# A hybrid decoder step: a hand-written order for the first stage, the first norm in column groups, and moved steps of the final norm

## The chip, the cores and the metric

One core of one Trainium2 chip, a program in Bass with the Tile framework. The time is device time in microseconds of one execution; the median of three runs of the kernel before is 1126.55 us (1126.41 to 1127.04). Engines: TensorE (PE), VectorE (DVE), ScalarE (ACT), GpSimd (POOL), SyncE (SP, which here only issues DMAs).

## What is computed

One layer, for 1024 prompt tokens and 8 x 8 sample tokens, 1088 columns in all; features lie on partitions, tokens in columns.

```
h = RMSNorm(x, g1);  proj = h @ w_in                  # 1024 -> 2816 + 8 columns (dt)
A = gelu(u) * (tril(W_s) gelu(v) + b)                 # chunks of 128 tokens
B = bgate * conv3(cgate * hb)
C = RMSNorm(ssd(silu(conv4(xbc)), softplus(dt)) * silu(z))
x = x + concat(A, B, C) @ w_out
x = x + relu(RMSNorm(x, g2) @ w_ff1)^2 @ w_ff2        # 1024 -> 4096 -> 1024
y = RMSNorm(x, final_norm)
```

## The kernel before, in words

Each float32 operand is split into a high part (a cast to fp32r) and a low part (what is left), and a product is three matmuls: high x high, low x high, high x low (`mm3`, L125 to L130, and `mm_tile`, L1039 to L1046). Columns go in chunks `CH` of 364, 364 and 360, later in quarters of 272.

**First stage.** Eight tiles of x^T (`xts`, 544 KB each) are loaded on SP's queue. For each k, `dt_products(k)` (L240) gives the eight dt columns, the high part of `g1 * x` is made on VectorE for k below 3 and on ScalarE above (L254, L256), the low part on VectorE (L259), the square on ScalarE (`square`, L229), and VectorE adds the squares up in `ss` (`add_square`, L233). The weight of an output tile is split by `split_w` (cast on ScalarE, L97; low part on VectorE, L98). The product of the first weight tile, over all three chunks at once, is L333 and L337. Its result goes to `cb` unscaled (L342). The second weight's `gemm` (L128 to L130) goes chunk by chunk; its first chunk has a PSUM tile of its own, and a hook behind it calls `rms_scale` (L155 to L181): three products of `ones` with `ss` (L169), Ln, Exp and one Newton step on all 1088 columns (L170 to L180), which gives `rstd` on all partitions. After that each result is multiplied with `rstd` when it leaves PSUM (`evac_pad`, L290), and so are the first tile's (L351) and dt (L355, L357). `dt_tokens` (L379) is hooked into the third weight's product, behind its first chunk. PSUM pool `gp` has three banks for the chunks.

**Order.** The text of the program is not the order on the engines: outside `manual_schedule` blocks a planner orders each engine's instructions by its own costs and due times, and fills gaps with later work that is ready. Inside a `manual_schedule(engines=...)` block the named engines run in the written order. In the kernel before there is one such block, around `last_products` (L1346 to L1349), for PE, DVE, ACT and POOL.

**Output projection.** `proj_out(t, f)` (L843) for two halves of the tokens and eight output tiles f, 48 matmuls each; `next_w` splits the weight one tile ahead. During the second half, behind the projections f = 1 to 4, the first half's norm is worked in: `norm_quarter(b, 0, ...)` (L904, four products of 544 columns on VectorE, L909) and `first_operand(n)` (L946, a split into a third of `big`, L914 and L915, and a write to DRAM on SP's queue). `first_operand(0)` needs only quarter (0, 0), `first_operand(1)` needs quarter (1, 0).

**The tail.** `last_products` (L1349) does the last second-layer product by column tiles and the final norm at once. `tile(c, j, m)` is six matmuls of 272 columns on TensorE, `put` (an addition into x on VectorE, L944) and a `square` on ScalarE (L1444). The tokens are done in three parts ci: 0 is the first half, 2 and 3 are quarters. For each part: `rms_mm` (sums of the squares over partitions, L870, four column groups of 32), `root_of` (Sqrt and Identity on ScalarE, L877 and L878; reciprocal and three more on VectorE, L879 to L882), `spread` (L893) of the row to all partitions, a copy of it on ScalarE (L1393, L1468), and the outputs: `weigh` (ScalarE, L1479) followed by `scale` on GpSimd (L1488) for f = 1, 5, 7, and `scale` on VectorE straight out of PSUM (L1493) for the others. `sum_2` and `sum_3` share a PSUM bank. A second product into `ca[m]` can begin only when the first one's `put` has read it.

Of the kernel before, what the change touches and what calls it, by code (L numbers as in the profile page):

```python
# [15 lines left out]
P = 128  # L16
# [52 lines left out]
def body(nc, tc, I, O):  # L69
# [24 lines left out]
    def split_w(st, cuts=(0, 1024), pool=None):  # L94
        w = (pool or whlp).tile([P, 2, 1024], F32R, name="whl")
        for a, b in zip(cuts, cuts[1:]):
            S.copy(out=w[:, 0, a:b], in_=st[:, a:b])  # L97
            V.tensor_tensor(out=w[:, 1, a:b], in0=st[:, a:b], in1=w[:, 0, a:b].bitcast(F32),  # L98
                            op=ALU.subtract)
        return w  # L100
# [9 lines left out]
    def w_split(i):  # L110
        if i < len(w_plan) and i not in w_sp:
            w_sp[i] = split_w(w_st[i], HC if i == 0 else (0, 1024))
# [134 lines left out]
    for k in range(KT):  # L247
        xt = xts[k]
        dt_products(k)
        b = big[:, k * 2 * T:(k + 1) * 2 * T].rearrange("p (h t) -> p h t", h=2)  # L250
        g = C("g1")[:, k:k + 1]
        for a, e in (((0, 364), (364, T)) if k == 0 else ((0, T),)):
            if k > 2:
                S.activation(out=b[:, 0, a:e], in_=xt[:, a:e], func=AF.Identity, scale=g)  # L254
            else:
                V.tensor_scalar(out=b[:, 0, a:e], in0=xt[:, a:e], scalar1=g, scalar2=None, op0=ALU.mult)  # L256
        if k == 0:
            w_split(0)
        V.scalar_tensor_tensor(out=b[:, 1], in0=xt[:, :T], scalar=g, in1=b[:, 0].bitcast(F32),  # L259
                               op0=ALU.mult, op1=ALU.subtract)  # L260
        if k:
            square(k - 1)
        if k > 2:
            add_square(k - 2)
        xg.append(b)
    w_split(1)
    square(KT - 1)
    add_square(KT - 2)
    add_square(KT - 1)
# [22 lines left out]
    S.copy(out=ones, in_=C("ones"))  # L292
# [47 lines left out]
    for c in range(3):  # L340
        for o, i, tok in pad_parts(buf, 3, ps0[c], c):
            S.copy(out=o, in_=i)  # L342
    dtT = tmpp.tile([P, T], F32, name="dtT", tag="t")[:, :DTQ + 32]
    S.copy(out=dtT[:, :DTQ], in_=psd[:, :DTQ])
    S.copy(out=dtT[:64, DTQ:], in_=psd[:64, DTQ:DTQ + 32])
    buf5 = new_buf(3, C("sst")[:, 5 * 24:6 * 24])
    gemm(next_w(), xg, range(KT), lambda c, ps: evac_pad(c, ps, buf5, 3),
         first=ap.tile([P, 512], F32, name="aps", tag="a"), hooks=[lambda: rms_scale(aslots(), catp, "yb", ss, rstd, D, False)])
    for c in range(3):
        for o, i, tok in pad_parts(buf, 3, ps0[c], c):  # L350
            V.tensor_tensor(out=o, in0=o, in1=tok(rstd), op=ALU.mult)  # L351
    conv_c(4, buf)
    for j in range(4):
        r = slice(32 * j, 32 * j + 32)
        V.tensor_tensor(out=dtT[r, :DTQ], in0=dtT[r, :DTQ], in1=rstd[r, j * DTQ:(j + 1) * DTQ], op=ALU.mult)  # L355
        if j < 2:
            V.tensor_tensor(out=dtT[r, DTQ:], in0=dtT[r, DTQ:], in1=rstd[r, SEQ + 32 * j:SEQ + 32 * j + 32],  # L357
                            op=ALU.mult)
    conv_c(5, buf5)
# [100 lines left out]
    V.tensor_tensor(out=ss, in0=rstd, in1=rstd, op=ALU.mult)  # L460
# [592 lines left out]
    for f in range(KT):  # L1053
# [12 lines left out]
        elif f == 2:  # L1066
            norm_quarter(1, 0, two(rstd[:, :NH]))
        elif f == 3:
            first_operand(0)
        elif f == 4:  # L1070
            first_operand(1)
# [277 lines left out]
    def last_products(fo, put):  # L1349
# [37 lines left out]
        for m in range(3):  # L1387
# [9 lines left out]
        tile(0, 3, 3)  # L1397
        scale(0, (0,))
        tile(1, 5, 0)
        rms_mm(2, sum_2)  # L1400
        scale(0, (2,))
        rs[2] = root_of(2, sum_2)
        tile(1, 5, 1)
# [5 lines left out]
        scale(0, (4,))  # L1409
        tile(1, 3, 1)  # L1410
# [4 lines left out]
        weigh(2, (1,))  # L1415
        tile(1, 3, 3)
        weigh(2, (5, 7))
# [198 lines left out]
```

## Time and profile before

| | |
|---|---|
| median of three runs | 1126.55 us |
| the profiled execution | 1127.05 us, span 1125.3 us |
| PE busy | 1111.0 us (99%) |
| DVE busy | 840.4 us (75%) |
| ACT busy | 497.8 us (44%) |
| POOL busy | 53.2 us (5%) |

Times in the rows are microseconds from the span's start. A matmul's time is pipelined: the next one starts before the last one's end. A name in the form L98 is a line of the kernel before. In a timeline row, what stands in square brackets is how long the engine sat idle before, and what it waited for.

### The profile page before, as it was taken

Reading aid. Unit: us, or ns where it says so; the run is one execution under the profiler, and the core shown is the slowest. Engines: PE = TensorE matmul, PEld = TensorE weight load, DVE = VectorE, ACT = ScalarE, POOL = GpSimd, SP = SyncE. Lnnn points to the kernel's source line nnn. Section 1 sums busy time; section 2 is a strip of 40 time slices with the busy share of each in tenths; the row PEclk is TensorE's granted clock in tenths of the full one; section 3 lists DMA queues with packets and bytes.
Section 4 is the critical chain, followed back from the end, with each engine's and each line's share of the span. In section 5 each row is a group of like instructions: output and inputs, shape, how many; then the busy total and the mean of one; then the engine's idle time right before and its main releaser. Section 6 shows DMA issues by size and latency. Waiting matters only on the chain.

```text
span 1125.3 us, 19943 instructions
## 1 busy us (share of the span) xinstructions
PE 1111.0 (99%) x8524; PEld 1090.8 (97%) x8524; DVE 840.4 (75%) x1111; ACT 497.8 (44%) x659; POOL 53.2 (5%) x89
## 2 busy tenths in 40 slices
PE   8999999999999999999999999999999999999996
PEld 6999999999999999999999999999999999999995
DVE  8875587865655477999697497596596596599786
ACT  7536273423553344653343443443443442543544
POOL 1110021110000000000000000000000000000014
PEclk9999999999999999999999999999999999999999
DMA  6112233321027263692853953953953953953504
GB/s 257 52 60 62 61 113 104 114 70 52 34 93 280 79 229 117 277 410 80 336 175 129 399 180 138 390 185 138 394 180 144 382 186 146 378 183 142 215 1 160
DMA packets 34776, 200.43 MB, mean 178 GB/s; under 512 B 4736, under 2 KB 7680, under 8 KB 27776
## 3 DMA queue, kind: packets, MB, share of 16 engines
q1 hardware_dynamic: 32592, 196.30, 47.2%
q10 hardware_dynamic: 2096, 2.85, 0.7%
q8 instruction: 67, 1.10, 0.4%
q14 instruction: 21, 0.17, 0.0%
HBM read 175.58 MB, written 22.77 MB: 176 GB/s over the span
## 4 chain that ended last, share of the span: by engine, by line
PE 94%; DVE 3%; issue 1%; ACT 1%; DMA 1%; POOL 0%; SPq 0%; POOLq 0%; DVEq 0%; ACTq 0%
PE ps L1045 20%; PE ps L1044 20%; PE ps L1046 20%; PE gps L128 10%; PE gps L129 9%; PE gps L130 9%; PE aps L574 1%; PE aps L578 1%; DMA xt<-xT 1%; DVE big L259 1%; DVE xq L909 0%; PE aps L509 0%; PE aps L505 0%; PE p L1044 0%; PE aps L767 0%
## 5 line engine op out<-in xcount | busy, mean ns | idle before, releaser
L1045 PE MATMUL ps<-big,whl 128*128 128x272 f32 x1312 | 377.7, 288 | 0.0
L1044 PE MATMUL ps<-big,whl 128*128 128x272 f32 x1312 | 377.5, 288 | 0.0
L1046 PE MATMUL ps<-big,whl 128*128 128x272 f32 x1312 | 376.9, 287 | 0.0
L1045 PEld LDWEIGHTS ps<-big,whl 128*128 128x128 f32 x1312 | 247.1, 188 | 0.2 <-issue 0.2
L1044 PEld LDWEIGHTS ps<-big,whl 128*128 128x128 f32 x1312 | 247.1, 188 | 0.2
L1046 PEld LDWEIGHTS ps<-big,whl 128*128 128x128 f32 x1312 | 246.8, 188 | 0.0
L128 PE MATMUL gps<-big,whl 128*128 128x360 f32 (+2 forms) x752 | 239.8, 319 | 0.5 <-ACT cb L342 0.5
L129 PE MATMUL gps<-big,whl 128*128 128x360 f32 (+2 forms) x752 | 236.8, 315 | 0.5 <-DVE whl L98 0.5
L130 PE MATMUL gps<-big,whl 128*128 128x360 f32 (+2 forms) x752 | 236.0, 314 | 0.0
L97 ACT CAST whl<-wq 128x1024 fp32r<-128x1024 f32 x92 | 96.6, 1051 | 220.7 <-PE ps L1046 132.9
L98 DVE TENSOR_TENSOR whl<-wq,whl 128x1024 fp32r<-128x1024 f32 x92 | 112.3, 1220 | 50.1 <-ACT whl L97 50.1
L128 PEld LDWEIGHTS gps<-big,whl 128*128 128x128 f32 x752 | 141.4, 188 | 2.0 <-ACT cb L342 1.0
L129 PEld LDWEIGHTS gps<-big,whl 128*128 128x128 f32 x752 | 141.4, 188 | 1.1 <-DVE whl L98 0.7
L130 PEld LDWEIGHTS gps<-big,whl 128*128 128x128 f32 x752 | 141.3, 188 | 0.1
L944 DVE TENSOR_TENSOR x<-x,ps 128x544 f32<-128x544 f32 x188 | 130.5, 713 | 7.8 <-PE ps L1046 6.7
L1046 PE MATMUL ps<-fo,whl 128*128 128x272 f32 x416 | 119.5, 287 | 0.0
L1044 PE MATMUL ps<-fo,whl 128*128 128x272 f32 x416 | 119.3, 287 | 0.0
L1045 PE MATMUL ps<-fo,whl 128*128 128x272 f32 x416 | 119.2, 287 | 0.0
L97 ACT CAST whl<-wst 128x1024 fp32r<-128x1024 f32 (+2 forms) x39 | 40.1, 1027 | 129.5 <-PE gps L130 81.0
L1044 PEld LDWEIGHTS ps<-fo,whl 128*128 128x128 f32 x416 | 78.3, 188 | 0.2 <-issue 0.2
L1046 PEld LDWEIGHTS ps<-fo,whl 128*128 128x128 f32 x416 | 78.2, 188 | 0.0
L1045 PEld LDWEIGHTS ps<-fo,whl 128*128 128x128 f32 x416 | 78.2, 188 | 0.0
(327 smaller groups left out, 1382.1 us busy)
## 6 DMA issues: line engine op xcount, KB each, us to landing
big<-xcd SPq DMA_DIRECT2D x47, 2176.0 KB, 9.7
wq<-w SPq DMA_DIRECT2D x66, 512.0 KB, 4.5
xcd<-big SPq DMA_DIRECT2D x7, 2176.0 KB, 8.1
wst<-w_in SPq DMA_DIRECT2D x21, 512.0 KB, 3.6
wst<-w_out SPq DMA_DIRECT2D x16, 512.0 KB, 3.6
x<-xT SPq DMA_DIRECT2D x8, 544.0 KB, 5.4
dec<-scr SPq DMA_DIRECT2D x8, 512.0 KB, 4.1
xt<-xT SPq DMA_DIRECT2D x7, 544.0 KB, 9.0
```

The source lines that it names most:

```text
L97: S.copy(out=w[:, 0, a:b], in_=st[:, a:b])
L98: V.tensor_tensor(out=w[:, 1, a:b], in0=st[:, a:b], in1=w[:, 0, a:b].bitcast(F32), op=ALU.subtract)
L128: PE.matmul(ps[:, :n], hi, xh, start=start, stop=False)
L129: PE.matmul(ps[:, :n], lo, xh, start=False, stop=False)
L130: PE.matmul(ps[:, :n], hi, xl, start=False, stop=stop)
L259: V.scalar_tensor_tensor(out=b[:, 1], in0=xt[:, :T], scalar=g, in1=b[:, 0].bitcast(F32), op0=ALU.mult, op1=ALU.subtract)
L574: PE.matmul(yps[hh * HD:(hh + 1) * HD, i * L:(i + 1) * L], w[:, h * HD:(h + 1) * HD], m[:, h], start=i == 0 and n == 0, stop=n == len(term ...
L578: PE.matmul(sps[:, g * 256:(g + 1) * 256], bt[:, g * P:(g + 1) * P], xw[:, g * 256:(g + 1) * 256], start=True, stop=True)
L944: V.tensor_tensor(out=out, in0=a, in1=b, op=o)
L1044: PE.matmul(o, hi, xh, start=start and k == 0, stop=False, skip_group_check=True)
L1045: PE.matmul(o, lo, xh, start=False, stop=False, skip_group_check=True)
L1046: PE.matmul(o, hi, xl, start=False, stop=k == ks - 1, skip_group_check=True)
```

## The change

1. First stage: VectorE and ScalarE are put in a `manual_schedule` block. All dt products stand first in the text; then high and low parts, with the sums of squares after the last low part except the square of k = 0 and 1; the second weight's split stands behind `add_square(1)` and `square(2)`. The copies of dt out of PSUM close the block.
2. First norm: the sums go as four column groups of 32 partitions with 364 columns each (the fourth repeats the third), Ln, Exp and the Newton step run on 364 columns, and three products with a column of `ident` spread the result over all partitions, behind the third chunk. The second weight's evacuations come after that; the scaling of dt stands ahead of that of the first tile.
3. The square of `rstd` goes from VectorE to ScalarE.
4. `first_operand(0)` stands behind projection 2 and `norm_quarter(1, 0)` behind projection 3, the reverse of before.
5. Tail: `tile(0, 3, 3)` ahead of the first spread; the sums of part 2 in two pieces, the second and `root_of(2)` behind `tile(1, 5, 1)`; the three weighings of part 2 together, behind `tile(1, 3, 0)`.

```diff
@@ -91,8 +91,9 @@
         SY.dma_start(out=st, in_=src)
         return st
 
-    def split_w(st, cuts=(0, 1024), pool=None):
-        w = (pool or whlp).tile([P, 2, 1024], F32R, name="whl")
+    def split_w(st, cuts=(0, 1024), pool=None, w=None):
+        if w is None:
+            w = (pool or whlp).tile([P, 2, 1024], F32R, name="whl")
         for a, b in zip(cuts, cuts[1:]):
             S.copy(out=w[:, 0, a:b], in_=st[:, a:b])
             V.tensor_tensor(out=w[:, 1, a:b], in0=st[:, a:b], in1=w[:, 0, a:b].bitcast(F32),
@@ -109,7 +110,7 @@
 
     def w_split(i):
         if i < len(w_plan) and i not in w_sp:
-            w_sp[i] = split_w(w_st[i], HC if i == 0 else (0, 1024))
+            w_sp[i] = split_w(w_st[i])
 
     def next_w():
 
@@ -245,28 +246,50 @@
                       start=k == 0 and o == 0, stop=k == KT - 1, skip_group_check=True)
 
     for k in range(KT):
-        xt = xts[k]
-        dt_products(k)
-        b = big[:, k * 2 * T:(k + 1) * 2 * T].rearrange("p (h t) -> p h t", h=2)
+        xg.append(big[:, k * 2 * T:(k + 1) * 2 * T].rearrange("p (h t) -> p h t", h=2))
+
+    def high(k):
         g = C("g1")[:, k:k + 1]
         for a, e in (((0, 364), (364, T)) if k == 0 else ((0, T),)):
+            o, i = xg[k][:, 0, a:e], xts[k][:, a:e]
             if k > 2:
-                S.activation(out=b[:, 0, a:e], in_=xt[:, a:e], func=AF.Identity, scale=g)
+                S.activation(out=o, in_=i, func=AF.Identity, scale=g)
             else:
-                V.tensor_scalar(out=b[:, 0, a:e], in0=xt[:, a:e], scalar1=g, scalar2=None, op0=ALU.mult)
-        if k == 0:
-            w_split(0)
-        V.scalar_tensor_tensor(out=b[:, 1], in0=xt[:, :T], scalar=g, in1=b[:, 0].bitcast(F32),
-                               op0=ALU.mult, op1=ALU.subtract)
-        if k:
-            square(k - 1)
-        if k > 2:
-            add_square(k - 2)
-        xg.append(b)
-    w_split(1)
-    square(KT - 1)
-    add_square(KT - 2)
-    add_square(KT - 1)
+                V.tensor_scalar(out=o, in0=i, scalar1=g, scalar2=None, op0=ALU.mult)
+
+    def low(k):
+        V.scalar_tensor_tensor(out=xg[k][:, 1], in0=xts[k][:, :T], scalar=C("g1")[:, k:k + 1],
+                               in1=xg[k][:, 0].bitcast(F32), op0=ALU.mult, op1=ALU.subtract)
+
+
+    ET = mybir.EngineType
+    with tc.manual_schedule(engines={ET.DVE, ET.Activation}):
+        for k in range(KT):
+            dt_products(k)
+        high(0)
+        low(0)
+        w_sp[0] = whlp.tile([P, 2, 1024], F32R, name="whl")
+        split_w(st0, HC[:2], w=w_sp[0])
+        square(0)
+        high(1)
+        low(1)
+        split_w(st0, HC[1:], w=w_sp[0])
+        high(2)
+        square(1)
+        low(2)
+        for k in range(3, KT):
+            high(k)
+            low(k)
+        add_square(1)
+        square(2)
+        w_split(1)
+        for k in range(2, KT):
+            if k > 2:
+                square(k)
+            add_square(k)
+        dtT = tmpp.tile([P, T], F32, name="dtT", tag="t")[:, :DTQ + 32]
+        S.copy(out=dtT[:, :DTQ], in_=psd[:, :DTQ])
+        S.copy(out=dtT[:64, DTQ:], in_=psd[:64, DTQ:DTQ + 32])
 
     def evac_mul(c, ps, dst, rhs=None):
         rhs = rstd if rhs is None else rhs
@@ -289,7 +312,6 @@
         for o, i, tok in pad_parts(buf, pad, ps, c):
             V.tensor_tensor(out=o, in0=i, in1=tok(rhs), op=ALU.mult)
 
-    S.copy(out=ones, in_=C("ones"))
     stC = sml.tile([P, 8, 27], F32, name="stC")
     xcS = sml.tile([P, 8, TS], F32, name="xcS")
     mids = {}
@@ -340,22 +362,45 @@
     for c in range(3):
         for o, i, tok in pad_parts(buf, 3, ps0[c], c):
             S.copy(out=o, in_=i)
-    dtT = tmpp.tile([P, T], F32, name="dtT", tag="t")[:, :DTQ + 32]
-    S.copy(out=dtT[:, :DTQ], in_=psd[:, :DTQ])
-    S.copy(out=dtT[:64, DTQ:], in_=psd[:64, DTQ:DTQ + 32])
+    S.copy(out=ones, in_=C("ones"))
     buf5 = new_buf(3, C("sst")[:, 5 * 24:6 * 24])
-    gemm(next_w(), xg, range(KT), lambda c, ps: evac_pad(c, ps, buf5, 3),
-         first=ap.tile([P, 512], F32, name="aps", tag="a"), hooks=[lambda: rms_scale(aslots(), catp, "yb", ss, rstd, D, False)])
-    for c in range(3):
-        for o, i, tok in pad_parts(buf, 3, ps0[c], c):
-            V.tensor_tensor(out=o, in0=o, in1=tok(rstd), op=ALU.mult)
-    conv_c(4, buf)
+
+    GRP = ((0, 364), (364, 364), (724, 364), (724, 364))
+    nrm = catp.tile([P, T], F32, name="nrm", tag="yb")
+    nr, nt = nrm[:, :364], nrm[:, 364:728]
+
+    def norm_sums():
+        sb = ap.tile([P, 512], F32, name="aps", tag="a")[:, :364]
+        for j, (c0, n) in enumerate(GRP):
+            PE.matmul(sb[32 * j:32 * j + 32], C("ones")[:, :32], ss[:, c0:c0 + n], start=True, stop=True,
+                      skip_group_check=True)
+        S.activation(out=nt, in_=sb, func=AF.Ln, bias=C("eps"), scale=1.0 / D)
+        V.tensor_scalar(out=sb, in0=sb, scalar1=1.0 / D, scalar2=EPS, op0=ALU.mult, op1=ALU.add)
+        S.activation(out=nr, in_=nt, func=AF.Exp, scale=-0.5)
+        V.tensor_tensor(out=nt, in0=nr, in1=nr, op=ALU.mult)
+        V.scalar_tensor_tensor(out=nt, in0=nt, scalar=-0.5, in1=sb, op0=ALU.mult, op1=ALU.mult)
+        V.scalar_tensor_tensor(out=nr, in0=nt, scalar=1.5, in1=nr, op0=ALU.add, op1=ALU.mult)
+
+    def norm_spread():
+        for j, (ps, (c0, n)) in enumerate(zip(aslots(), CH)):
+            PE.matmul(ps[:, :364], C("ident")[:, 32 * j:32 * j + 1].broadcast_to([P, P]), nr, start=True, stop=True)
+            S.copy(out=rstd[:, c0:c0 + n], in_=ps[:, 364 - n:364])
+
+    held = []
+    gemm(next_w(), xg, range(KT), lambda c, ps: held.append((c, ps)), first=ap.tile([P, 512], F32, name="aps", tag="a"),
+         hooks=[norm_sums, lambda: None, norm_spread])
+    for c, ps in held:
+        evac_pad(c, ps, buf5, 3)
     for j in range(4):
         r = slice(32 * j, 32 * j + 32)
         V.tensor_tensor(out=dtT[r, :DTQ], in0=dtT[r, :DTQ], in1=rstd[r, j * DTQ:(j + 1) * DTQ], op=ALU.mult)
         if j < 2:
             V.tensor_tensor(out=dtT[r, DTQ:], in0=dtT[r, DTQ:], in1=rstd[r, SEQ + 32 * j:SEQ + 32 * j + 32],
                             op=ALU.mult)
+    for c in range(3):
+        for o, i, tok in pad_parts(buf, 3, ps0[c], c):
+            V.tensor_tensor(out=o, in0=o, in1=tok(rstd), op=ALU.mult)
+    conv_c(4, buf)
     conv_c(5, buf5)
 
 
@@ -457,7 +502,7 @@
 
     stB = sml.tile([P, 2, 18], F32, name="stB")
     catB = []
-    V.tensor_tensor(out=ss, in0=rstd, in1=rstd, op=ALU.mult)
+    S.activation(out=ss, in_=rstd, func=AF.Square)
 
     def proj_b(i):
         cg = tmpp.tile([P, T], F32, name="cg", tag="t")
@@ -1064,9 +1109,9 @@
                 S.copy(out=rstd[:, CQ[c]], in_=ps[:, :NQ])
             norm_quarter(0, 0, two(rstd[:, :NH]))
         elif f == 2:
+            first_operand(0)
+        elif f == 3:
             norm_quarter(1, 0, two(rstd[:, :NH]))
-        elif f == 3:
-            first_operand(0)
         elif f == 4:
             first_operand(1)
     pps.close()
@@ -1384,7 +1429,7 @@
         add_up(2, top)
         token_sums(sum_a, (ss[:, HALF[0]], sq_of(0, 0)))
         rs[0] = root_of(0, sum_a)
-        for m in range(3):
+        for m in range(4):
             tile(0, 3, m)
             if m < 2:
                 weigh(0, ((1,), (5,))[m])
@@ -1394,27 +1439,26 @@
         scs[0] = rstd[:, HALF[0]], spa[:, :, :NQ]
         weigh(0, (7,))
         scale(0, (1, 5, 7))
-        tile(0, 3, 3)
         scale(0, (0,))
         tile(1, 5, 0)
-        rms_mm(2, sum_2)
+        rms_mm(2, sum_2, (8, 0, 1, 2), True, False)
         scale(0, (2,))
+        tile(1, 5, 1)
+        rms_mm(2, sum_2, (3,), False, True)
         rs[2] = root_of(2, sum_2)
-        tile(1, 5, 1)
         tile(1, 5, 2)
         scale(0, (3,))
         tile(1, 5, 3)
         add_up(3, top)
         tile(1, 3, 0)
         scale(0, (4,))
+        weigh(2, (1, 5, 7))
         tile(1, 3, 1)
         tile(1, 3, 2)
         spread_to(2, one())
         rms_mm(3, sum_3, (0, 1), True, False)
         scale(0, (6,))
-        weigh(2, (1,))
         tile(1, 3, 3)
-        weigh(2, (5, 7))
         rms_mm(3, sum_3, (8, 2, 3), False, True)
 
         for u in range(N_WARM):
```

## Rows read from the trace of the kernel before

**Rows 1.** The page, part 1: busy time, share of the span and instructions of each engine.

```profile
PE 1111.0 (99%) x8524; PEld 1090.8 (97%) x8524; DVE 840.4 (75%) x1111; ACT 497.8 (44%) x659; POOL 53.2 (5%) x89
```

**Rows 2.** The waits of TensorE, by its line and by what it waited for: us in total, times, longest.

```profile
PE aps L244 <- DMA xt<-xT: 1.7, 1, 1.7
```

**Rows 3.** Two stretches of the whole: length, then busy time and instructions of each engine, granted clock, DMA share, GB/s.

```profile
8.06:25.27 17.21, 17.21 (x154) 14.11 (x154) 17.07 (x15) 14.94 (x15) 2.28 (x2) 1.00 0.75 302
...
409.39:1095.75 686.36, 685.87 (x5490) 684.92 (x5488) 537.97 (x618) 294.47 (x344) 4.11 (x3) 1.00 0.59 223
```

**Rows 4.** Timeline of TensorE from 24.6 to 27.1 us: start, us, engine, line.

```profile
24.61 0.66 PE L333 MATMUL gps<-big,whl 128*128 128x364 f32 x3
25.11 0.33 PE L128 MATMUL aps<-big,whl 128*128 128x364 f32 x1
25.97 0.80 PE L128 MATMUL gps<-big,whl 128*128 128x364 f32 x2 [0.53 <-ACT cb L342]
26.75 0.43 PE L129 MATMUL aps<-big,whl 128*128 128x364 f32 x1
27.02 0.33 PE L130 MATMUL aps<-big,whl 128*128 128x364 f32 x1
```

**Rows 5.** Timeline of VectorE in the first stage.

```profile
12.90 3.86 DVE L259 SCALAR_TENSOR_TENSOR big<-xt,cp,big 128x1088 fp32r<-128x1088 f32 x3
...
23.02 1.34 DVE L259 SCALAR_TENSOR_TENSOR big<-xt,cp,big 128x1088 fp32r<-128x1088 f32 x1
...
25.49 1.21 DVE L98 TENSOR_TENSOR whl<-wst,whl 128x1024 fp32r<-128x1024 f32 x1
26.62 2.67 DVE L233 TENSOR_TENSOR ss<-ss,xt 128x1088 f32<-128x1088 f32 x2
```

**Rows 6.** The loads of x and ScalarE's part of the first stage: the issues of six tiles on SP's queue; the DMA view of the last two issues, with KB each and us from issue to landing; ScalarE's timeline.

```profile
2.61 3.98 SPq L220 DMA_DIRECT2D xt<-xT  x6
...
xt<-xT SPq DMA_DIRECT2D x2, 544.0 KB, 10.6
...
18.71 2.28 ACT L254 ACTIVATE big<-xt,cp 128x1088 fp32r<-128x1088 f32 x2
20.90 2.20 ACT L229 ACTIVATE xt<-xt 128x1088 f32<-128x1088 f32 x2
23.01 1.03 ACT L97 CAST whl<-wst 128x1024 fp32r<-128x1024 f32 x1
```

**Rows 7.** Timeline of TensorE at the first norm's sums. Each float32 product shows as two records.

```profile
30.69 1.99 PE L169 MATMUL aps<-ss,cp 128*128 128x364 f32 x6
...
32.69 0.33 PE L130 MATMUL gps<-big,whl 128*128 128x364 f32 x1
```

**Rows 8.** Timeline of TensorE at the second norm: sums in column groups of 32 and the matmul after next, then the spread and the matmul after next.

```profile
389.90 0.44 PE L870 MATMUL aps<-ss,cp 128*32 128x136 f32 x8
...
390.50 0.29 PE L129 MATMUL gps<-big,whl 128*128 128x272 f32 x1
...
396.36 1.09 PE L893 MATMUL aps<-ss,cp 128*128 128x136 f32 x8
...
397.41 0.29 PE L129 MATMUL gps<-big,whl 128*128 128x272 f32 x1
```

**Rows 9.** Timelines at 44 us: TensorE, and VectorE's scaling of dt.

```profile
43.99 0.33 PE L130 MATMUL gps<-big,whl 128*128 128x364 f32 x1
44.56 0.83 PE L379 MATMUL aps<-cp,dtT 128*128 128x8 f32 x6 [0.23 <-DVE dtT L355]
...
43.65 0.85 DVE L355 TENSOR_TENSOR dtT<-dtT,rstd 32x256 f32<-32x256 f32 x2
```

**Rows 10.** Timelines at 409 us: TensorE, then VectorE.

```profile
409.26 0.28 PE L128 MATMUL gps<-big,whl 128*128 128x272 f32 x1
410.03 0.39 PE L129 MATMUL gps<-big,whl 128*128 128x272 f32 x1 [0.48 <-DVE whl L98]
...
405.98 2.86 DVE L909 SCALAR_TENSOR_TENSOR xq<-x,cp,rstd 128x544 f32<-128x544 f32 x4
408.76 1.21 DVE L98 TENSOR_TENSOR whl<-wst,whl 128x1024 fp32r<-128x1024 f32 x1
```

**Rows 11.** Timeline of VectorE in the tail: first scale, put, root of part 2, puts.

```profile
1105.56 0.78 DVE L1493 SCALAR_TENSOR_TENSOR yo<-x,cp,ps 128x544 f32<-128x544 f32 x1 [0.78 <-ACT rstd L1393]
1106.26 0.43 DVE L944 TENSOR_TENSOR x<-x,p 128x272 f32<-128x272 f32 x1
1106.61 0.77 DVE L1493 SCALAR_TENSOR_TENSOR yo<-x,cp,ps 128x544 f32<-128x544 f32 x1
1107.45 0.58 DVE L879 RECIPROCAL ss<-ss 128x68 f32<-128x68 f32 x1
...
1108.85 0.77 DVE L944 TENSOR_TENSOR x<-x,p 128x272 f32<-128x272 f32 x2
```

**Rows 12.** Timeline of ScalarE in the tail: a square and the copy of rstd; weighings and the last Sqrt.

```profile
1104.62 0.41 ACT L1444 ACTIVATE sq<-x 128x272 f32<-128x272 f32 x1
1104.93 0.59 ACT L1393 COPY rstd<-ps 128x544 f32<-128x544 f32 x1
...
1114.67 0.92 ACT L1479 ACTIVATE yo<-x,cp 128x272 f32<-128x272 f32 x2
1115.50 0.30 ACT L877 ACTIVATE ss<-ps,cp 128x68 f32<-128x68 f32 x1
```

## The prediction

> **What bounds the kernel now.** The page's first part came first: TensorE is busy for 1111.0 of 1125.3 us, VectorE for 75% [rows 1]. So 14.3 us at most lie outside TensorE's work, and a change that leaves that work alone can only take from these; a matmul added to TensorE counts in full. Next the waits of TensorE, of which the longest, 1.7, is for the second x tile [rows 2], and the stages: between 8.06 and 25.27 us TensorE is busy for all 17.21, and between 409 and 1096 us for 685.87 of 686.36, one matmul of 272 columns every 0.125 us [rows 3]. What the first stage's VectorE is late with therefore does not show before 25.27; the reader should look at what comes right after it, then at the three other places where the diff meets a wait: 44, 409 and 1095 to 1118 us.
>
> **First stage, the stall at 25 us.** After the last product of the first weight tile TensorE issues one matmul of the second tile, two early ones of other chunks, and goes on only at 26.75 [rows 4]. Three matmuls of 364 columns take 0.50, so 0.167 each; between 25.11 and 27.02 it does four of them, 0.67 us of work in 1.91: **1.24 lost**. It waited for VectorE's low half of the second weight tile (25.49, 1.21 long), which stood behind the last `low` (23.02) and sums of squares [rows 5]. In the written order the lows are not interrupted by sums. The last of the six x tiles is issued by 6.6 and lands some 10.6 later, near 17.2; its high half takes 1.2 on ScalarE, so it is ready near 18.4 and not at 21.0 [rows 6]. Lows at 1.26 apiece (12.90, three in 3.86, [rows 5]) keep up with that, so `low(7)` ends near 19.7; one sum (1.28) and the weight's low half (1.21) end near 22.1. Even if the second weight tile came no sooner than its cast ran before (23.01, [rows 6]), its low half would be there at 25.3. I take the whole 1.24 as gained, and keep 0 as the other end.
>
> **What the sums then cost.** The other sums come behind: six adds at 1.38 (26.62, two in 2.67, [rows 5]) from 21.9 end near 30.1, against 29.3 before (26.62 + 2.67). The squares are at ScalarE's 1.10 [rows 6] and are done by 25.7. TensorE, 1.24 earlier, ends the first chunk of the second product at 25.27 + 24 x 0.167 = 29.3, and the norm's sums are hooked there. If TensorE's sequence keeps them there it waits 0.8; if the planner, which still orders TensorE, sees the sum late, other chunks' matmuls go first and it waits nothing, as it already did with the two early matmuls [rows 4]. I take 0, and keep 0.8 as an end.
>
> **The norm on TensorE.** Removed: three full sums, from 30.69 to 32.69 less one matmul, 1.83 for six passes, 0.305 a pass of 364 columns [rows 7]. Added: four sums in column groups. For 136 columns such a group takes 0.60 less one matmul of 0.125 = 0.48; four separate 136-column products take 1.05 - 0.125 = 0.92, 0.115 a pass [rows 8]. So the groups run side by side and pay two passes: for 364 columns 0.48 + 2 x (0.305 - 0.115) = 0.86. Also added: three spreads, six passes, 1.83. **Net 0.86 more.** The matmuls are plain busy time of the bounding engine and nothing covers them. The Trainium skill, TensorEngine Tiling (Array Packing), Key Properties, says that changing the tiling mode drains TensorE, and its speedup table says up to 4 times for a dimension of 32; by the 4 times alone the sums would cost two passes, 0.61, and the stage would be 0.25 better. The row of the 136 columns decides: 0.48 where two passes are 0.23, so the switch does cost.
>
> VectorE loses the root over all 1088 columns, and ScalarE gains three copies; TensorE is packed in the stages behind [rows 3], so this is worth only the **wait at 44**: 43.99 + 0.17 to 44.56, 0.40, for the scaled dt [rows 9]. Now the spread stands behind the third chunk (29.3 + 0.86 + 8.0 = 38.1) and takes 1.83; the last copy ends near 40.6, the last chunk's evacuation and the dt products (the large four at 0.43, [rows 9]) follow, near 43 for a need at 40.0 + 4.0 = 44.0. I take 0.40 gained, 0 as the other end. The table loads before the logarithm and the exponential stay; they lie beside TensorE's chunks. The square of rstd that goes from VectorE to ScalarE, the copy of `ones` and the exchanged order of the convolutions are covered by an engine that TensorE does not wait for; uncovered they would be about 1.1, once. Stage: -1.24 - 0.40 + 0.86 = **-0.78**.
>
> **The quarter's norm.** At 409.26 TensorE waits until 410.03 for a low half of a weight: 0.77 less 0.125, **0.65** [rows 10]. VectorE did the four products of `norm_quarter(1, 0)` first (405.98, 2.86) and the split at 408.76. One projection later the norm stands behind that split in the program. Its operand is needed only after the projections, and its write to DRAM goes behind it on SP's queue, ahead of a weight load that has a projection (6 us) of slack. The next split could meet the same 2.86; it is ready earlier than the norm's input, so I take -0.65, with 0 as the other end.
>
> **The tail.** This order is written out for all engines, so it can be walked. VectorE's first `scale` of 544 columns starts at 1105.56 because it waits for ScalarE's copy of rstd (1104.93, 0.59) [rows 11, 12]. Now a fourth square (0.31, from 1104.62 to 1104.93 for the one there is) stands ahead of the copy: scale at 1105.9. Behind it VectorE has put, scale, put (0.35, 0.70, 0.35 from the starts in [rows 11]) where before only put and scale came ahead of the root: the second put starts at 1107.65 and ends at 1108.1. Its square on ScalarE (0.34) is ahead of the root's Sqrt, which starts at 1108.4, so the reciprocal runs at 1108.75 and not 1107.45. VectorE is free 1.40 later, 1110.15 against 1108.85 [rows 11], with one put (0.35) already done: 0.95 late. Everything behind is in order on it. Ahead of the square behind `tile(1,3,1)` ScalarE now does three weighings of 0.41 [rows 12], which adds some 0.6, and TensorE's sums of that square stand ahead of `tile(1,3,3)`, which so starts near 1114.3 (an estimate from these steps). Tile with restart and drain (six matmuls 0.75, plus about 0.3), put 0.43, square 0.43, sums 0.3: the last Sqrt starts at 1116.7. Before it started at 1115.50, straight behind two weighings that are now gone from there [rows 12]; that is in the 1116.7. What TensorE saves by filling its wait at 1102 is lost again by waiting for VectorE. After the Sqrt nothing changes. **+1.2**; ends -0.1 (next rival) and +1.5.
>
> **Sum.** -0.78 - 0.65 + 1.2 = -0.23 on the profiled execution's 1127.05 (span 1125.3 and 1.75 around it), so 1126.8; the median stands 0.50 under that execution: **1126.3**. About 0.2%, 2.25 us, is what a measurement of this kernel can tell from no change.
>
> **Rivals.** (B) *The tail does not slip.* If the scale did not wait for the copy it would start near 1103.6, after VectorE's fourth put, the root would come at its old place, and the last Sqrt near 1115.4: tail -0.1, sum -1.5, **1125.0**. Against it: the row names the copy as what ended the wait. The Trainium skill, PSUM — Partial Sum Buffer, "PSUM bank collisions raise a hardware error", asks that two engines' accesses to one bank be kept apart by semaphores, reads too; by that rule the scale waits for the copy in the new order as well, and the start at 1105.56 agrees. 0.15. With it, or without, TensorE may also fill the wait of 1.7 for the second x tile at 6.4 [rows 2] with six matmuls (1.0) whose inputs are there: -2.5, **1124.0**; the order of VectorE up to there stays the same, so only 0.06. (C) *The early gain is eaten:* the sums wait their 0.8 at 29.3, and the split at 409 is late again: 0.02 + 0 + 1.2, **1127.8**. For it, the hook is tied to the first chunk. 0.15. (D) *Slower.* The dt products of all eight x tiles are now written ahead of every split. If TensorE's sequence follows that and holds the first product back until the eighth x tile, landed at 17.2, its 72 matmuls (12.0) begin near 17.9 and end at 29.9 instead of 25.27: +4.6 less the 1.24 that then has no place, no 0.8, so 4.6 - 1.24 - 0.40 + 0.86 - 0.65 + 1.2, **1130.9**. It decides whether TensorE multiplies between 9 and 17 us. Against it: the dt products were ahead of that product in the program before too, and TensorE was packed [rows 3]. 0.04. That the change does not do what it says is in (C): only VectorE and ScalarE are written out in the first stage.
>
> **Numbers.** Forecast 0.60, B 0.15 and 0.06, C 0.15, D 0.04. The likeliest is 1126.3; 1124.8 to 1128.0 leaves out D, the 1124.0 and part of the ends. Faster 0.07, same 0.89, slower 0.04.
>
> **What would show it.** Right: no wait of TensorE between 25 and 27 and at 44 and 409; eight grouped sum records and six spread records of 364 columns; in the tail the reciprocal of the third part near 1108.7 less the 1.4 won earlier, and a `tile(1,3,3)` that starts after a wait for ScalarE's square. Wrong: a tail (from the start of its first column tile, 1095.75 here [rows 3], to the last Sqrt) no longer than 19.75 us, a wait at 29, or a first product that ends later than 25.3.

## The result and the profile after

| | before | after |
|---|---|---|
| median, 11 runs each on one chip | 1126.54 us | 1129.3 us |
| profiled execution, its span | 1127.05, 1125.3 | 1129.52, 1127.7 |
| ratio after to before | | 1.0021, 95% interval 1.0014 to 1.0029 |

The change made the kernel 2.76 us slower; the forecast was 0.2 faster. The profiled executions differ by 2.47 (spans 1125.26 and 1127.73), which the traces share out as follows, by when TensorE reaches the same matmul: -0.38 up to the second product (the second x tile landed earlier), **+0.91 in the first stage** (80.56 - 25.11 = 55.45 before, 81.09 - 24.73 = 56.36 after), **-0.73** at the quarter's norm, **+2.59 in the tail**, and 0.1 in small drifts. The first number is luck: the second product starts anywhere between 24.42 and 25.41 in the fifteen profiles, with either front.

First stage, TensorE and then VectorE. It answers to [rows 4, 7, 9].

```profile
24.73 0.33 PE L129 MATMUL aps<-big,whl 128*128 128x364 f32 x1
24.89 0.33 PE L130 MATMUL aps<-big,whl 128*128 128x364 f32 x1
...
33.61 0.82 PE L375 MATMUL aps<-ss,cp 128*32 128x364 f32 x8
34.36 0.43 PE L131 MATMUL gps<-big,whl 128*128 128x360 f32 x1
...
37.47 0.33 PE L131 MATMUL gps<-big,whl 128*128 128x360 f32 x1
38.65 2.10 PE L386 MATMUL aps<-nrm,cp 128*128 128x364 f32 x6 [0.85 <-DVE nrm L382]
...
54.27 0.23 PE L429 MATMUL aps<-cp,dtT 64*32 64x8 f32 x4
55.07 0.40 PE L129 MATMUL gps<-big,whl 128*128 128x364 f32 x1 [0.57 <-ACT whl L98]
...
29.48 1.28 DVE L234 TENSOR_TENSOR ss<-ss,xt 128x1088 f32<-128x1088 f32 x1
...
38.05 0.54 DVE L382 SCALAR_TENSOR_TENSOR nrm<-nrm 128x364 f32<-128x364 f32 x1
...
43.72 1.50 DVE L402 TENSOR_TENSOR cb<-cb,rstd 128x364 f32<-128x364 f32 x4
46.66 7.81 DVE L329 SCALAR_TENSOR_TENSOR xc<-cb,cp,xc 128x1112 f32<-128x1112 f32 x6 [1.45 <-ACT xc L326]
54.40 0.97 DVE L313 TENSOR_TENSOR cb<-gps,rstd 128x364 f32<-128x364 f32 x2
```

The stall of 1.24 at 25 us is gone, and so is the wait at 44. Two new ones stand at 38 and 55: the spread waits 0.85 for the Newton step, and the fourth weight's product waits 0.57. The wait row of 55.07 names a weight cast as the releaser, and that is wrong: the cast ends at that moment, but it is for a later weight. The other thing that ends just before is the first of VectorE's two L313 of 54.40, which empties the PSUM bank that the product needs (e_bank tests it).

Quarter's norm, VectorE; it answers to [rows 10]. The weight's low half now precedes the products of the norm, and TensorE has no wait between 400 and 440 us.

```profile
406.41 1.22 DVE L99 TENSOR_TENSOR whl<-wst,whl 128x1024 fp32r<-128x1024 f32 x1
...
410.25 0.78 DVE L954 SCALAR_TENSOR_TENSOR xq<-x,cp,rstd 128x544 f32<-128x544 f32 x1
```

Tail: VectorE, ScalarE and TensorE, to [rows 11, 12], then TensorE's stretches with the granted clock as the first decimal number behind the five engines.

```profile
1105.62 0.78 DVE L1537 SCALAR_TENSOR_TENSOR yo<-x,cp,ps 128x544 f32<-128x544 f32 x1 [2.25 <-ACT rstd L1438]
...
1108.49 0.58 DVE L924 RECIPROCAL ss<-ss 128x68 f32<-128x68 f32 x1 [0.70 <-ACT ss L922]
...
1112.08 1.33 ACT L1523 ACTIVATE yo<-x,cp 128x272 f32<-128x272 f32 x3
1113.32 0.73 ACT L1488 ACTIVATE sq<-x 128x272 f32<-128x272 f32 x2
...
1117.09 0.32 ACT L922 ACTIVATE ss<-ps,cp 128x68 f32<-128x68 f32 x1 [0.64 <-PE ps L915]
...
1110.38 0.40 PE L1089 MATMUL p<-big,whl 128*128 128x272 f32 x1 [0.82 <-DVE x L989]
...
1111.76 1.11 PE L938 MATMUL p<-ss,cp 128*128 128x68 f32 x8 [0.38 <-DVE x L989]
...
1113.78 0.33 PE L915 MATMUL ps<-sq,cp 128*32 128x68 f32 x8 [0.65 <-ACT sq L1488]
1114.04 0.39 PE L1089 MATMUL p<-big,whl 128*128 128x272 f32 x1
...
1118.97 1.98 PE L938 MATMUL p<-ss,cp 128*128 128x68 f32 x8
```

```profile
1108.00:1114.00 6.00, 4.14 (x43) 3.41 (x41) 5.08 (x12) 3.68 (x12) 3.91 (x5) 1.00 0.60 224
...
1114.30:1114.40 0.10, 0.10 (x2) 0.10 (x2) 0.00 (x0) 0.01 (x1) 0.01 (x1) 0.78 1.12 435
1114.40:1115.00 0.60, 0.60 (x5) 0.60 (x4) 0.00 (x0) 0.00 (x0) 0.60 (x1) 0.50 0.99 356
```

Scale, reciprocal and `tile(1,3,3)` (1114.04) are where the prediction had them, less the 0.26 by which the tail began early. But between 1108 and 1114 TensorE is now idle for 1.86 of 6 us, in three waits, where before it was never idle in that stretch; and at 1114.36 its clock falls to 1.2 GHz. From there its matmuls of 272 columns come every 0.225 us and the eight spread records take 1.98 instead of 1.11. In the kernel before TensorE is busy for all 6.00 of that stretch, and the clock stayed at 2.4 GHz until TensorE's last work was done:

```profile
1108.00:1114.00 6.00, 6.00 (x75) 5.62 (x73) 5.01 (x14) 3.03 (x8) 4.26 (x6) 1.00 0.69 257
1114.00:1118.00 4.00, 2.38 (x38) 1.88 (x26) 3.49 (x10) 2.90 (x8) 1.89 (x3) 1.00 0.86 306
```

### The profile page after: what moved, and what is told of

It is laid out like the page before. It is cut to its first block, busy times and chain, and to the rows that moved or that the text cites. A ratio compares the mean times of both kernels' runs of the same rounds, so it can differ in the third digit from the quotient of the medians.

```text
span 1127.7 us, 19953 instructions
## 1 busy us (share of the span) xinstructions
PE 1114.4 (99%) x8532; PEld 1093.1 (97%) x8532; DVE 836.2 (74%) x1102; ACT 498.6 (44%) x661; POOL 48.3 (4%) x89
## 4 chain that ended last, share of the span: by engine, by line
PE 96%; ACT 1%; DVE 1%; issue 1%; DMA 1%; POOL 0%; SPq 0%; POOLq 0%; DVEq 0%; ACTq 0%
PE ps L1090 20%; PE ps L1089 20%; PE ps L1091 19%; PE gps L129 10%; PE gps L130 10%; PE gps L131 10%; PE aps L619 1%; PE aps L623 1%; PE gps L355 1%; DMA xt<-xT 1%; PE gps L359 0%; PE aps L245 0%; PE aps L554 0%; PE aps L550 0%; PE aps L812 0%
```

## The experiments

Two lengths of the trace are compared, since they agree between profiles far better than whole times do. **S** is the first stage: from the first matmul of the second product to its kind counted 100 later in the products. **T** is the tail: from the start of its first column tile to the start of the last Sqrt, and to the start of the last spread matmul.

**Which part costs?** Three kernels take parts away.

```diff
 a_tailb: the changed kernel, last_products as before
 b_tail:  the kernel before, last_products as changed
 b_first: the kernel before, first stage and square of rstd as changed
```

> The changed kernel with the tail in the order of before; first stage and quarter's norm as changed. Theory (the loss is in the tail: 2.6 us, of which some 1.2 are the waits behind VectorE and ScalarE and 1.4 the fall of the granted clock to 1.2 GHz at 1114.36): 0.28 us under before, 1126.2 to 1126.5, last TensorE work at full clock. Rival (the first stage, or something that it leaves, makes the tail late whatever its order): within 0.7 of the changed kernel, 1128.6 or more.

> The kernel before with the new tail alone. Theory: 2.6 us over before, 1129.1, with the clock at 1.2 GHz from about 0.3 us after the first sums of the third part on. If the waits alone come with the order and the clock fell for another reason: 1.2 over, 1127.7. Rival (the tail is innocent): 1126.5.

> The kernel before with the first stage alone (written order, norm by column groups, square of rstd on ScalarE). Theory from the two traces (+0.9 from the first product to 390 us, -0.4 from an earlier x tile): 0.4 to 0.5 over before, 1127.0. As the prediction had it: 0.78 under, 1125.8. The difference to the kernel with all but the new tail is the quarter's norm: theory and prediction both 0.65 to 0.73.

Measured beside before at 1126.88: a_tailb 1127.39 (ratio 1.0006, 0.9997 to 1.0015), b_tail 1129.74 (1.0021, 1.0012 to 1.0029), b_first 1127.97 (1.0012, 1.0004 to 1.0021). The tail alone makes a loss as large as the whole one. S is 56.37 in a_tailb and b_first, 0.92 over before each time, so the first stage is slower too, by twice what the theory wrote (the 0.38 of the x tile was luck). a_tailb missed its number by that, and by a tail 0.28 longer than the one of before (see the end). The quarter's norm is a_tailb less b_first: 0.58 in medians.

**The clock in the tail.** The changed tail, its idle waits filled with useless matmuls in two ways.

```diff
 a_fill, into a free half of the sums' PSUM tile:
+        fill(8)            # ahead of tile(1, 3, 2); 4, 5 and 3 at the next waits
 a_pad, zeros added to the column tile's own sum:
-        tile(1, 3, 1)
-        tile(1, 3, 2)
+        tile(1, 3, 1, 6)   # six matmuls of zeros at its end
+        tile(1, 3, 2, 3)
```

> The changed kernel with 20 matmuls of 272 columns, whose result nothing reads, in the four idle waits of TensorE in the tail (8 ahead of the third column tile of part 3, 4 ahead of the spread, 5 between the first two sums, 3 ahead of the last two). Theory (the clock fell because TensorE stood idle at 1109 to 1114): the clock stays at 2.4 GHz to the last spread and 1.2 to 1.4 us come back, 1127.9. Rival (the clock falls in the tail anyway, or for a reason that more matmuls make worse): 1129.3 or up to 1 us more, since at 1.2 GHz the added matmuls no longer fit in the waits.

> The changed kernel with nine matmuls of zeros (272 columns, bf16) at the ends of the second and third column tile of the last round, which fill the two waits at 1109 and 1111 us without a wait of their own. Theory (the fall of the clock follows those idle waits and is worth 1.4 to 2 us; the waits behind VectorE alone cost the 1.2 of the prediction): clock at 2.4 GHz to the last spread, part 2's Sqrt at 12.67 and the last Sqrt at 21.0 to 21.3 from the tail's start, last spread at 23.7 to 24.0 (25.04 in the changed kernel), 1.0 to 1.3 over the kernel before and with little scatter. Rival (the clock does not hang on these waits): spread at 25, 2 or more over before.

| | part 2's Sqrt | T to last Sqrt | T to last spread | clock at last spread | time (before) |
|---|---|---|---|---|---|
| before | 11.37 | 19.75 | 22.45 | 2.4 GHz | |
| a_tailb | 11.65 | 20.03 | 22.73 | 2.4 | 1127.39 (1126.88) |
| after | 12.67 | 21.60 | 25.04 | 1.2 | 1129.3 (1126.54) |
| b_tail | 12.69 | 22.01 | 25.45 | 1.2 | 1129.74 (1126.88) |
| a_fill | 12.67 | 21.66 | 24.38 | 2.4 | 1129.18 (1126.88) |
| a_pad | 12.67 | 21.01 | 23.72 | 2.4 | 1128.4 (1127.08) |

In a_fill the clock stayed up, but the time hardly fell: its first added matmuls had to wait 0.48 for VectorE's root, which uses the same PSUM tile, and pushed `tile(1,3,3)` 0.64 later. In a_pad that tile starts at the same 18.55 as in the changed kernel, and the lengths come out as the theory had them (the time is 1.32 over before, just above its 1.0 to 1.3):

```profile
1111.57 0.52 PE L1425 MATMUL p<-zb 128*128 128x272 bf16 x3
...
1114.37 0.39 PE L1089 MATMUL p<-big,whl 128*128 128x272 f32 x1
...
1118.71 1.11 PE L938 MATMUL p<-ss,cp 128*128 128x68 f32 x8 [0.81 <-DVE ss L927]
```

```profile
1118.00:1120.00 2.00, 1.11 (x8) 0.97 (x8) 1.40 (x5) 0.72 (x3) 0.00 (x0) 1.00 0.44 156
```

So the waits cost 1.26 (21.01 - 19.75), and the clock 1.32 more (25.04 - 23.72). Against a_tailb, which has the order of before and its last Sqrt at 20.03, the waits cost 0.98: with the first stage as changed, the tail of before is itself 0.28 longer (see the end). The ratio of a_pad is 1.0012 (1.0003 to 1.0021).

Single executions say the same. With the waits left open, the mean granted clock of an execution is 0.993 or 0.994 in 7 of 11 of b_tail and in 6 of 11 of the changed kernel; with the waits filled it is 0.997 or more in all 22 of a_pad and a_fill. The four of b_tail with 0.997 to 0.998 took 1127.69 to 1128.80, the seven others 1129.72 to 1130.58. One execution of the changed kernel (1130.34) and one of a_pad (1130.23) were long at 0.997; that is not explained.

The tail of before is not safe either: in the profile of b_first, which has it, the clock fell at 1118.68, inside the last spread, whose last matmul starts at 23.31 instead of the 22.75 of e_bank.

**Which step of the tail?** One at a time, put back in the changed kernel: the root of part 2, the weighings, the copy of rstd.

```diff
 t_root
-        rms_mm(2, sum_2, (8, 0, 1, 2), True, False)
+        rms_mm(2, sum_2)
         scale(0, (2,))
+        rs[2] = root_of(2, sum_2)
         tile(1, 5, 1)
-        rms_mm(2, sum_2, (3,), False, True)
-        rs[2] = root_of(2, sum_2)
 t_weigh
-        weigh(2, (1, 5, 7))
...
+        weigh(2, (1,))
         tile(1, 3, 3)
+        weigh(2, (5, 7))
 t_copy
+        square(2, (3,))    # behind the copy of rstd, no longer in tile(0, 3, 3)
         weigh(0, (7,))
```

> The changed kernel with the sums and the root of part 2 back in one piece behind the first column tile of the last round; the early fourth tile and the joined weighings stay. Measured from the start of the tail's first column tile to part 2's Sqrt and to the last Sqrt (before 11.37 and 19.75, changed kernel 12.67 and 21.60). Theory (the late root makes VectorE 0.95 late, TensorE idles behind it at 1109 to 1114, and the clock falls for that): part 2's Sqrt at 11.4 to 11.7, the last Sqrt at 20.0 to 20.4, the clock at 2.4 GHz to the last spread, and a time 1.2 to 1.8 under the changed kernel's, 1127.5 to 1128.1. Rival (the joined weighings are what makes the last sums late): 21 or more, within 0.6 of the changed kernel.

> The changed kernel with the three weighings of part 2 back in their two places (one ahead of the last column tile, two behind it). Theory: they moved the square ahead of the last sums by some 0.6, but without them there two weighings stand ahead of the last Sqrt again (0.8); last Sqrt at 21.2 to 21.7, time within 0.5 of the changed kernel's 1129.3. Rival (the weighings are the cause): last Sqrt at 20.4 or less, 1128.1 or less.

> The changed kernel with the copy of part 0's rstd ahead of the fourth square. Theory (my step: the scale waits for the copy, and the copy for that square): the first scale of 544 columns starts 0.3 earlier (9.83 from the same start, against 10.13 in the changed kernel), part 2's Sqrt and the last Sqrt 0.3 earlier too, 12.4 and 21.3, time 0.3 to 0.5 less, 1128.9; more only where the clock no longer falls. Rival (the copy is not on the path): Sqrt at 12.67, no change.

Beside before at 1127.26: t_root 1128.23 (1.0011, 1.0002 to 1.0020), part 2's Sqrt 11.97, last Sqrt 20.67, clock up; t_weigh 1128.62 (1.0012, 1.0003 to 1.0021), last Sqrt 20.72, the clock down from 1118.53, 0.1 into the last spread; t_copy 1129.29 (1.0017, 1.0008 to 1.0026), part 2's Sqrt 12.35, last Sqrt 21.66, clock down. The copy's step is the 0.3 of the prediction at part 2's Sqrt; at the last Sqrt the clock, down from 1113.50, hides it. The root and the weighings are worth 0.3 each at the last Sqrt (against 21.01 in a_pad). Both theories missed: t_root should have reached 20.4 and stays at 20.67, t_weigh should have come down to 21.2 only and reaches 20.72. If the copy's 0.3 went through to the last Sqrt, which no run shows, the three would make 0.9 of the 1.26 (or of the 0.98 against a_tailb). None is the cause alone.

**The first stage.** Written order or column groups alone; then two mends of the changed stage: the sums earlier on TensorE, and a PSUM bank of its own for the fourth product's first chunk. All five have the tail of before and the changed quarter's norm, e_cols too: its edit also swaps `first_operand(0)` and `norm_quarter(1, 0)`, so its expectation, which calls it the column groups alone, leaves out some 0.7 that it gains at 410 us. S ends long before that.

```diff
 e_sums: the second product in written order on TensorE
+    with tc.manual_schedule(engines={ET.PE}):
...
+                mm3(ps, w1, k, xg[k], c0, n, k == 0, k == KT - 1)
+                if (c, k) == (1, 4):
+                    norm_sums()
 e_bank: in proj_c
+        first = ap.tile([P, 512], F32, name="aps", tag="a") if i == 7 else None
 e_both: both
 e_order: rms_scale of before, and its order of scalings, behind the written block
 e_cols: norm_sums and norm_spread in the order of before
```

> The changed kernel with the tail of before, and TensorE in written order in the second weight's product: the norm's four sums stand behind 15 of the 24 matmuls of the second chunk (about 31.2 us) instead of where they were put (33.6). Measure: from the first matmul of that product to the hundredth triple of the products, 56.37 us with the changed first stage, 55.45 before. Theory A (the spread waits 0.85 for the root because the sums come late, and nothing else holds): no wait at the spread, no wait at 55, 54.7, and 1.7 us less in all. Theory B (VectorE's chain of evacuations, scalings and convolution up to 54.4 is the next bound): the wait at the spread goes, but the one at 55 for a free PSUM bank grows by as much, 56.2 to 56.4.

> The changed kernel with the tail of before, and a PSUM bank of its own for the first chunk of the fourth weight's product, which otherwise waits for VectorE's evacuation of the third product's first chunk, behind six convolution steps (7.81 us, to 54.47). Theory (the wait of 0.6 to 0.7 at 55 is for that bank): no wait there, 55.66 by the measure of the run before (56.37 less 0.71). Rival (it waits for the weight's cast, which the view of waits names): unchanged, 56.37.

> Both edits together, with the changed first stage and quarter's norm and the tail of before. Under theory A as under B the two waits go: 56.37 less 1.0 and 0.71, 54.7 by the same measure, 0.75 less than before (the prediction's sum for this stage was -0.78), and 1.4 us less than the kernel before in all: 1125.3 to 1125.6. If it is no better than the kernel before, something in the stage still costs that I have not named.

> The changed kernel with the tail of before and with the norm of before (full-width sums, Newton step on 1088 columns), so the written order alone. As the prediction costed the order: 1.24 less at 25 us and nothing back, 54.2 by the same measure, 1126.1 in all with the quarter's 0.7. Theory from the trace of the changed kernel (the sums of squares end 1.4 us later and the norm's sums come 2.9 us later than before, while TensorE is 1.2 us ahead): the wait for the scaled dt at 44 grows from 0.4 to 3 or more and the stage is 1.5 to 3 us slower than before, 57 to 58.4.

> The kernel before with the norm by column groups alone (and the square of rstd on ScalarE), in the order of before. By the prediction's terms, without those of the written order: 0.86 more on TensorE less the 0.40 of the wait for dt, 55.9 by the measure from the second product's start to the hundredth triple (55.45 before), total 0.46 over before. Rival (the sums come late here too and the spread waits about 1.0): 56.9, 1.4 over.

| | S | waits of TensorE from 25 to 57 us | time (before), ratio |
|---|---|---|---|
| before | 55.45 | at 25 and 44 | |
| changed stage | 56.36 | spread 0.85, bank 0.57 | |
| e_order | 59.73 | banks 3.4 in two, dt 0.5 | 1131.28 (1127.11), 1.0037 (1.0023 to 1.0050) |
| e_cols | 57.27 | at 25, bank 1.25 | 1128.43 (1127.08), 1.0012 (1.0003 to 1.0021) |
| e_sums | 56.03 | bank 1.25 | 1126.99 (1127.11), 0.9999 (0.9990 to 1.0008) |
| e_bank | 55.76 | spread 0.86 | 1126.85 (1127.11), 0.9997 (0.9988 to 1.0006) |
| e_both | 54.76 | none | 1126.10 (1127.11), 0.9991 (0.9982 to 1.0000) |

e_bank removes the wait at 55 without touching a cast: the product starts at 55.04 while the cast of that time (54.64, 1.05 long) still runs, so the releaser named in the view of waits was the wrong one. e_sums decides for theory B: the spread's wait goes, but the bank's grows from 0.57 to 1.25, because VectorE's chain up to 54.4 hardly moves (its evacuation starts at 54.31; against the start of S that is 0.34 earlier, which is what S gains). Only both mends together bring the stage under before, by 0.69, and e_both is 1.0 us under the kernel before, at the edge of its interval, and some 3.8 under the changed one, each measured against its own before. It has the tail of before, so only the first stage and the quarter's norm of the change are left in it. It fell short of its forecast by some 0.4; its trace shows a start 0.2 later and a tail 0.3 longer than before's. Its rows of TensorE, where the two waits were:

```profile
38.08 0.32 PE L131 MATMUL gps<-big,whl 128*128 128x360 f32 x1
38.24 2.00 PE L387 MATMUL aps<-nrm,cp 128*128 128x364 f32 x6
39.80 0.61 PE L129 MATMUL gps<-big,whl 128*128 128x364 f32 x1
...
53.86 0.23 PE L439 MATMUL aps<-cp,dtT 64*32 64x8 f32 x4
54.02 0.43 PE L129 MATMUL aps<-big,whl 128*128 128x364 f32 x1
```

The written order with the norm of before is the worst of all: S is 4.3 over before, more than its expectation's 1.5 to 3, and the wait that grew is the one for banks, not the one for dt. Its sums start late as well (33.54, before 30.69), and with the full-width root the same chain on VectorE ends at 56.2 (convolution to 55.2, a weight's low half, then the bank). Some 1.7 of the 4.3 are the clock, not waits: behind its long wait it is down from 57.16 to 60.58, and TensorE, busy throughout, does half the work in these 3.42 us (an estimate from these rows). e_cols missed both its numbers of S: the column groups in the order of before bring no wait at the spread but the same wait of 1.25 for the bank. The long wait of e_order:

```profile
53.77 0.23 PE L404 MATMUL aps<-cp,dtT 64*32 64x8 f32 x4
56.91 0.42 PE L129 MATMUL gps<-big,whl 128*128 128x364 f32 x1 [2.91 <-DVE cb L313]
```

## Why the prediction was wrong

The forecast was 1126.3 and the measured median 1129.3. By the traces the first stage makes 1.7 of the miss and the clock in the tail 1.3; the early x tile, which is luck, takes 0.4 off.

**First stage, predicted -0.78, measured +0.91: the step that failed is "worth only the wait at 44", with its cover "an engine that TensorE does not wait for".** What was counted held: -1.24 at 25, -0.40 at 44, and TensorE's net of +0.86 is near what the rows give (the sums hold the next matmuls back by 0.93, from 33.36 to 34.63 less two matmuls; e_both's S is 0.69 under before). Two waits were missing. First, the sums. The prediction let the other chunks' matmuls go ahead of them and put the wait at nothing. For the sums that is right; but they started at 33.61, not at 29.3, and the root takes 5.0 us from there to 38.59 (Ln at 34.50, then a table load of 1.28, Exp at 36.37, three VectorE steps). The spread was due at 37.64 and came at 38.65: +1.0. The prediction never set the root's length against the matmuls in front of the spread. Second, the exchange of scalings and convolutions. With the evacuations held until the spread and dt ahead of the first tile's scaling, ScalarE's opening step of the convolution starts at 45.31 (before 42.74), VectorE sits idle 1.45 for it, and its six convolution steps start at 46.66 (before 44.53). The next evacuation behind them frees a bank that TensorE needs: from the last small product to the next matmul 0.80 instead of 0.16, +0.64. Sum: -1.24 - 0.40 + 0.86 + 1.0 + 0.64 = 0.86 against 0.91. The prediction priced that exchange, with the square and the copy of `ones`, at 1.1 "uncovered" and dropped it. A slip beside it changed nothing: the adds' 1.38 is 1.34 by the row that it names.

**Quarter's norm, -0.65: right** (-0.73 in the trace; 0.58 in medians).

**Tail, +1.2, measured +2.59: the waits were right, and the step that failed is "After the Sqrt nothing changes".** The waits that the prediction itself forecast let the clock fall while work was left. That adds 1.32 in the trace of an execution in which it falls, and about 2 between the executions of b_tail; a_pad, with the waits filled, is 1.26 over before at the last Sqrt. The walk up to `tile(1,3,3)` came out to within 0.1 us, once the early start of the tail is taken off. Its end has two slips: VectorE is free 1.30 later by its own times, not 1.40 (the 0.95 that it goes on with is right), and the terms behind 1114.3 add up to 1116.5, not 1116.7, so to +1.0. The nearness of +1.2 to a_pad's 1.26 is therefore in part luck.

**The signs.** None of the three signs of being wrong came (a tail no longer than 19.75, a wait at 29, a late first product), and those of being right did, but for the 1.4 that the tail was to begin earlier by. They were set on the places that the prediction had looked at; the two new waits and the clock stood elsewhere.

**Rivals.** B is refuted: the scale did wait for the copy (1105.62). C had the right side of the first stage but the wrong place; there is no wait at 29. D is refuted: the first product ends on time. No rival had the spread's wait, the wait for the bank or the lower clock.

## What to carry to other kernels

When a reduction is shortened by spreading its result back, set the whole chain (sums, tables, root) against the work that stands between, from the place where the planner will put the sums, not from the hook. When evacuations are held back, look which later product needs their PSUM banks, and what long block on the evacuating engine now stands in front of them. A new idle wait on TensorE near the end may have to be priced twice: here its own length was 1.26 us, and the work behind it at half the clock another 1.32, which 13 of the 22 executions of b_tail and the changed kernel paid.

## What was not expected of the hardware

- The clock fell in the changed tail after three waits of 0.4 to 0.8 us with work between them, 1.86 us idle in 6; in e_order it fell once in the first stage, at 57.16 after a single wait of 2.91, and was back at 60.58:

```profile
57.50:60.00 2.50, 2.50 (x10) 2.50 (x9) 1.74 (x4) 2.47 (x5) 1.31 (x3) 0.50 0.60 206
60.00:62.00 2.00, 2.00 (x12) 2.00 (x11) 1.90 (x5) 1.98 (x2) 0.00 (x0) 0.86 0.91 252
62.00:70.00 8.00, 8.00 (x51) 8.00 (x50) 7.51 (x24) 1.42 (x2) 0.55 (x3) 1.00 0.01 3
```

- The Trainium skill, TensorE: Matmul & The Clock Gate, section "What's actually happening", says that the low clock is the default and that activity releases it. The rows agree (0.50 once the waits of the tail had come, 1.00 again in e_order at 60.58, with TensorE busy since its wait), and so does a_pad: nine matmuls of zeros kept the clock up. The mean clock says that it fell early in 7 of 11 executions of b_tail and not in the others; why is open.
- Left open too: with the tail of before, part 2's Sqrt comes at 11.65 in six profiles (a_tailb, b_first, e_sums, e_bank, e_both, e_cols), at 11.37 in the kernel before and at 11.40 in e_order. The six have the norm in column groups and the two others do not; the written order and the quarter's norm do not bring it, since e_order has both. That is one profile of each, and how a norm at 34 us should reach the tail is open. It begins at the first square of the last round, which starts 0.09 after its input is written in the kernel before and in e_order and 0.37 after it in a_tailb. With the changed tail there is no such difference (12.69 in b_tail, 12.67 in the changed kernel).
